# Merging logits and PV items of an attention stage by another weight

## The chip, the cores and the metric

The kernel runs on one core of a Trainium2 chip. The metric is the time of one execution in microseconds (us) on the device; of several executions the median counts. TensorE does the matmuls, VectorE, ScalarE and GpSimd the elementwise work, SyncE (SP) issues the DMAs.

## The reference: what is computed

One layer of a decoder on 2048 tokens of width 1024, with 16 learned meta tokens ahead of them. RMSNorm and one input projection feed three causal mixers: latent attention (MLA, 6 heads, keys of 64 + 32 rotary), differential attention (diff, 4 heads, two softmax maps of width 32 each per head, their weighted difference is applied to the values) and a sliding window of 128 (6 heads). Their outputs go through one output projection and the residual, then RMSNorm, a SwiGLU FFN of width 2816, the residual and a last RMSNorm:

```python
y = concat(mla(...), diff(...), swa(...))          # each (2048, heads * 64)
h = h + y @ w_out
h = h + (silu(n @ w_gate) * (n @ w_up)) @ w_down   # n = rms_norm(h)
out = rms_norm(h)[meta:]
```

For MLA and diff, a query row block of 128 attends to all key blocks up to its own, and to the meta tokens: softmax(q k + bias) v.

## The kernel before, in words

The program has four phases: phase_a projects, phase_b does MLA and diff attention, phase_o does the window attention and the output projection, phase_f the FFN. They overlap at their borders. Numbers are kept as pairs of a rounded part and its rest, so that two or three matmuls stand for one exact product.

**A unit of phase_b** is a pair of query row blocks (2g and 2g+1, g from 0 to 7) of one head. There are 48 MLA units; 32 diff units are spread over them, so that of three steps of the outer loop (`for j in range(48)`, end of phase_b) two carry a diff unit beside the MLA unit (a mixed unit below; unit 0 is the first step). Each unit gives two lists of work items, s1 (logits) and s2 (PV).

**Logits** (softmax_row). A row of 128 queries has its keys cut into pieces of 144 to 512 columns. For a piece, TensorE computes the logits into one of three PSUM buffers psS: three matmuls for MLA (lines 744 to 746), one for diff (line 802). VectorE then adds the bias, writes the piece into an SBUF tile p and keeps the running minimum mn (line 574), which frees psS. After a row's last piece ScalarE takes the exponentials of the whole row (line 579), and for diff GpSimd combines the two maps (lines 788 and 789). A diff unit has four such rows (two blocks, two maps), an MLA unit two. There are 12 p tiles.

**PV** (pv_pair). For two key blocks at a time TensorE transposes p into a PSUM buffer psTb (line 612, three buffers), ScalarE rounds it to pth (line 623) and VectorE forms the rest ptl (line 624); every third time ScalarE, then GpSimd do it (lines 619 to 621). Then TensorE multiplies both by the values into psO (line 642). A close folds and scales the sum (lines 649, 754, 755, 811 to 816) and stores y.

**Order.** PV of a unit is written into the program together with the logits of the next one. merge_to does it: each list's items have weights, and the list that is behind in its share of its own total gives the next item. With `merge(s1, prev)` the PV items of the unit before (prev) are so spread over the logits pieces. Of the PV items the weights are fixed (0.22 per transposed pair of blocks and the like). In a mixed unit, the rows of MLA and diff are first merged the same way, each row with the sum of its pieces' weights (rows_of, then merge_to).

The order written isn't yet the order that runs. The framework orders the instructions of each engine at build time along its own model of time (`TCKW = dict(schedule_with_timeline_sim=True)`, line 36): among those that the model holds ready, the one written first goes first.

Of the kernel before, what the change touches and what calls it, by code (L numbers as in the profile page):

```python
# [88 lines left out]
def key_chunks(m):  # L89

    out, c = [], 0
    for b in ([m] if m <= 8 else [-(-m // 2), m // 2]):
        w = b * P + (0 if c else META)
        n = -(-w // PW)
        pieces = []
        for j in range(n):
            k = (b // n + (1 if j >= n - b % n else 0)) * P + (0 if c else META)
            pieces.append((c, k))
            c += k
        out.append(pieces)  # L100
    return out
# [3 lines left out]
def trunk(ctx: ExitStack, tc: tile.TileContext, a, out):  # L105
# [408 lines left out]
    def phase_b(window):  # L514
        with ExitStack() as st:
# [28 lines left out]
            def softmax_row(items, i, mm_fn, cost, bias, fin):  # L544


                chunks = key_chunks(i + 1)
                last = chunks[-1][-1]
                st_ = {"n": 0, "p": []}

                def part(j, c0, w, e):
                    if e == 0:
                        st_["ps"] = psS.tile([P, PW], F32, name="psS")
                    ps = st_["ps"]
                    if w <= 512:
                        lo, hi = PW - 512, PW - 512 + w
                        mm_fn(ps[:, lo:hi], c0, w)
                    else:
                        w0 = w // 2 // 8 * 8
                        lo, hi = 512 - w0, 512 + w - w0  # L560
                        if e == 0:
                            return mm_fn(ps[:, lo:512], c0, w0)
                        mm_fn(ps[:, 512:hi], c0 + w0, w - w0)
                    n = st_["n"]
                    st_["n"] += 1
                    if n == 0:
                        st_["mn"] = sm.tile([P, 8], F32, name="mn")
                    mn = st_["mn"]
                    base = chunks[j][0][0]
                    if c0 == base:  # L570
                        st_["p"].append((base, chunks[j][-1][0] + chunks[j][-1][1] - base, pp.tile([P, CH], F32, name="p", bufs=NPB)))
                    p = st_["p"][j][2]
                    b = bias[:, 512 - w:512] if (c0, w) == last else zero.to_broadcast([P, w])
                    nc.vector.tensor_tensor_reduce(out=p[:, c0 - base:c0 - base + w], in0=ps[:, lo:hi], in1=b, scale=1.0,  # L574
                                                   scalar=mn[:, n - 1:n] if n else 3e38, op0=ALU.add, op1=ALU.min, accum_out=mn[:, n:n + 1])
                    if (c0, w) == last:
                        rsum = sm.tile([P, 2], F32, name="rsum")
                        for k, (_, m, x) in enumerate(st_["p"]):
                            nc.scalar.activation(out=x[:, 0:m], in_=x[:, 0:m], func=AF.Exp, bias=mn[:, n:n + 1], scale=-1.0, accum_out=rsum[:, k:k + 1])  # L579
                        if len(chunks) > 1:  # L580
                            nc.gpsimd.tensor_tensor(out=rsum[:, 0:1], in0=rsum[:, 0:1], in1=rsum[:, 1:2], op=ALU.add)
                        fin(st_["p"], rsum[:, 0:1])

                for j, pieces in enumerate(chunks):
                    for c0, w in pieces:
                        c = max(w, 256) * cost / 2400.0
                        if w > 512:
                            items.append((c / 2, lambda j=j, c0=c0, w=w: part(j, c0, w, 0)))
                            items.append((c / 2, lambda j=j, c0=c0, w=w: part(j, c0, w, 1)))
                        else:  # L590
                            items.append((c, lambda j=j, c0=c0, w=w: part(j, c0, w, 0)))
                items.append((0.0, lambda: None))
# [139 lines left out]
            def mla_unit(h, g, q, hf, kt, vt):  # L732
                s1, s2 = [], []
                rows, sums = [], []

                def fin(p, s):
                    rows.append(p)
                    sums.append(s)

                for i in (2 * g, 2 * g + 1):  # L740
                    o = slice((i - 4 * hf) * P, (i - 4 * hf + 1) * P)

                    def qk(s, c0, w, o=o):
                        nc.tensor.matmul(out=s, lhsT=q[:, 0, o], rhs=kt[:, c0:c0 + w], start=True, stop=False)
                        nc.tensor.matmul(out=s, lhsT=q[:, 1, o], rhs=kt[:, c0:c0 + w], start=False, stop=False)
                        nc.tensor.matmul(out=s, lhsT=q[:, 2, o], rhs=kr[:, c0:c0 + w], start=False, stop=True)

                    softmax_row(s1, i, qk, 3, ncaus[:, 4], fin)

                def out_y(yp):  # L750
                    y = tp.tile([P, 2, 64], F32, name="y")
                    r = sm.tile([P, 2], F32, name="ri")
                    for j in range(2):
                        nc.vector.reciprocal(out=r[:, j:j + 1], in_=sums[j])
                    nc.vector.tensor_tensor(out=y, in0=yp.rearrange("p (j d) -> p j d", j=2), in1=r.unsqueeze(2).to_broadcast([P, 2, 64]), op=ALU.mult)
                    nc.sync.dma_start(out=y_v[:, 2 * g:2 * g + 2, h * 64:(h + 1) * 64], in_=y)

                pv_pair(s2, g, rows, vt, out_y)
                return s1, s2
# [14 lines left out]
            def diff_unit(h, g, q, hf, kt, vt):  # L774
# [23 lines left out]
                for i in (2 * g, 2 * g + 1):  # L798
                    o = slice((i - 4 * hf) * P, (i - 4 * hf + 1) * P)
                    for m in range(2):  # L800
                        def qk(s, c0, w, o=o, m=m):
                            nc.tensor.matmul(out=s, lhsT=q[:, m, o], rhs=kt[m][:, c0:c0 + w], start=True, stop=True)  # L802
                        softmax_row(s1, i, qk, 1, ncaus[:, h], fin)
# [712 lines left out]
```

## Time and profile before

| | |
|---|---|
| median of 3 runs | 2818.74 us (2812.42 to 2819.20) |
| profiled execution | 2810.05 us |
| its span, first to last instruction | 2808.3 us |
| mean granted TensorE clock | 0.988 |
| TensorE busy with matmuls / loading weights | 2724.7 / 2339.2 us |
| VectorE, ScalarE, GpSimd busy | 1794.5, 1450.3, 1309.9 us |
| phase_b, first logits to first logits of unit 47 | 483 to 1105 us |

Busy time is the union of an engine's instructions. PE is TensorE's matmuls, PEld its weight loads, which overlap matmuls; DVE is VectorE, ACT ScalarE, POOL GpSimd. An idle stretch is put down to the instruction that released it: "PEld psS L802 <- DVE mn L574" is the weight load of line 802 that waited for line 574 on VectorE. Idle time of an engine costs something only where nothing else sets the pace there.

### The profile page before, as it was taken

What the parts mean: (1) busy time and instruction counts of PE and PEld (TensorE: products, weight loads), DVE (VectorE), ACT (ScalarE), POOL (GpSimd) and SP (SyncE); (2) the same over time, 40 slices, a digit from 0 to 9 for tenths busy, and PEclk for the clock granted to TensorE, in tenths of its full rate; (3) what the DMA queues carried; (4) which work ended last, traced back from release to release, by engine and by line L of the source; (5) the groups of instructions that cost most, each with busy time, mean ns of one, the idle gap of its engine ahead of it and who ended that gap; (6) DMA issues with size and microseconds to landing.
All of it is one profiled execution on the core that took longest, in us unless ns stands there. A gap on an engine that the chain in (4) does not pass through costs nothing.

```text
span 2808.3 us, 44596 instructions
## 1 busy us (share of the span) xinstructions
PE 2724.7 (97%) x14755; PEld 2339.2 (83%) x14755; DVE 1794.5 (64%) x4092; ACT 1450.3 (52%) x3264; POOL 1309.9 (47%) x1585
## 2 busy tenths in 40 slices
PE   8999999899999999899998999999999999999999
PEld 6888888888989899788886888887888888788887
DVE  6343333798988989655548666668766666655564
ACT  6444444788888888645444333334333333333343
POOL 1212122688887978512215555455654553222231
PEclk9999999899999999899999999999999999999999
DMA  7565456946464542667658333235322324834554
GB/s 198 144 179 141 136 145 170 246 99 152 117 159 101 135 100 66 187 180 212 182 170 263 107 104 109 90 98 202 113 96 95 107 91 140 309 120 144 174 189 147
DMA packets 418504, 415.53 MB, mean 148 GB/s; under 512 B 56426, under 2 KB 309328, under 8 KB 416352
## 3 DMA queue, kind: packets, MB, share of 16 engines
q1 hardware_dynamic: 418272, 412.67, 49.9%
q8 instruction: 117, 1.92, 0.3%
q14 instruction: 115, 0.94, 0.1%
HBM read 278.72 MB, written 137.18 MB: 148 GB/s over the span
## 4 chain that ended last, share of the span: by engine, by line
PE 81%; DMA 6%; DVE 4%; issue 4%; POOL 2%; ACT 2%; SPq 1%; POOLq 0%; DVEq 0%; ACTq 0%
PE ps L1225 10%; PE ps L1224 10%; PE ps L1223 10%; PE psO L642 5%; PE psA L123 4%; PE psTb L612 4%; PE psA L125 4%; PE psA L124 4%; PE ps L125 4%; PE ps L123 4%; PE ps L124 4%; PE psAo L123 2%; PE psAo L125 2%; PE psAo L124 2%; PE psS L802 2%
## 5 line engine op out<-in xcount | busy, mean ns | idle before, releaser
L1224 PE MATMUL ps<-x,wgh 128*128 128x512 f32 x1232 | 485.8, 395 | 4.8 <-DVE x L1193 4.8
L1223 PE MATMUL ps<-x,wgh 128*128 128x512 f32 x1232 | 483.6, 393 | 3.9 <-ACT x L1192 3.6
L1225 PE MATMUL ps<-x,wgl 128*128 128x512 f32 x1232 | 485.0, 394 | 2.2 <-DVE wgl L1215 2.2
L1155 POOL TENSOR_TENSOR wsum<-r 128x512 f32<-128x512 f32 x220 | 317.7, 1448 | 334.7 <-DVE wgl L1215 331.6
L579 ACT ACTIVATE p<-p,mn 128x656 f32<-128x656 f32 (+8 forms) x336 | 305.3, 914 | 34.9 <-DVE mn L574 30.3
L1214 ACT CAST wgh<-wsum 128x512 fp32r<-128x512 f32 x220 | 136.3, 620 | 311.0 <-PE ps L1224 199.3
L1224 PEld LDWEIGHTS ps<-x,wgh 128*128 128x128 f32 x1232 | 232.1, 188 | 61.7 <-DVE x L1193 8.8
L1223 PEld LDWEIGHTS ps<-x,wgh 128*128 128x128 f32 x1232 | 232.4, 189 | 57.9 <-ACT x L1192 4.4
L1225 PEld LDWEIGHTS ps<-x,wgl 128*128 128x128 f32 x1232 | 232.3, 189 | 53.8 <-DVE wgl L1215 2.6
L123 PE MATMUL ps<-bh,wgh 128*128 128x512 f32 x616 | 241.1, 394 | 2.6 <-ACT wgh L1360 2.6
L124 PE MATMUL ps<-bl,wgh 128*128 128x512 f32 x616 | 242.7, 394 | 0.0
L125 PE MATMUL ps<-bh,wgl 128*128 128x512 f32 x616 | 239.1, 395 | 0.0
L1215 DVE TENSOR_TENSOR wgl<-wsum,wgh 128x512 fp32r<-128x512 f32 x220 | 191.7, 872 | 58.8 <-ACT wgh L1214 57.5
L612 PE MATMUL psTb<-ident,p 128*128 128x128 f32 x1440 | 216.7, 276 | 3.5 <-DVE ptl L624 1.4
L123 PE MATMUL psA<-wi,xh 128*128 128x512 f32 (+2 forms) x528 | 203.4, 385 | 5.5 <-ACT wi L238 4.7
L1360 ACT CAST wgh<-wgl 128x512 fp32r<-128x512 f32 x154 | 95.0, 620 | 216.6 <-DMA wgl<-fd 180.9
L1361 DVE TENSOR_TENSOR wgl<-wgl,wgh 128x512 fp32r<-128x512 f32 x154 | 117.9, 773 | 132.6 <-ACT wgh L1360 127.9
L124 PE MATMUL psA<-wi,xh 128*128 128x512 f32 (+2 forms) x528 | 199.7, 378 | 0.4 <-DVE wi L239 0.3
L125 PE MATMUL psA<-wi,xl 128*128 128x512 f32 (+2 forms) x528 | 198.3, 376 | 0.0
L642 PE MATMUL psO<-pth,vt 128*128 128x256 f32 x720 | 193.4, 289 | 2.2 <-DMA vt<-vd 1.9
L642 PE MATMUL psO<-ptl,vt 128*128 128x256 f32 x720 | 194.1, 298 | 0.8 <-DVE ptl L624 0.2
L1155 POOL TENSOR_TENSOR hs<-c 128x512 f32<-128x512 f32 x108 | 154.9, 1441 | 61.5 <-DVE c L1314 51.9
(255 smaller groups left out, 6826.5 us busy)
## 6 DMA issues: line engine op xcount, KB each, us to landing
wgl<-fd SPq DMA_DIRECT2D x154, 256.0 KB, 3.4
fd<-hs SPq DMA_DIRECT2D x110, 256.0 KB, 2.8
qm<-qd SPq DMA_DIRECT2D x92, 256.0 KB, 5.0
r<-in_w_gate_dram SPq DMA_DIRECT2D x88, 256.0 KB, 4.1
r<-in_w_up_dram SPq DMA_DIRECT2D x88, 256.0 KB, 3.8
ws<-in_w_down_dram SPq DMA_DIRECT2D x77, 256.0 KB, 3.3
qd<-so SPq DMA_DIRECT2D x80, 192.0 KB, 2.0
qf<-qd SPq DMA_DIRECT2D x60, 256.0 KB, 5.6
```

Source lines behind the costliest of these rows:

```text
L123: nc.tensor.matmul(out=ps, lhsT=xh, rhs=wh, start=start, stop=False)
L124: nc.tensor.matmul(out=ps, lhsT=xh, rhs=wl, start=False, stop=False)
L125: nc.tensor.matmul(out=ps, lhsT=xl, rhs=wh, start=False, stop=stop)
L579: nc.scalar.activation(out=x[:, 0:m], in_=x[:, 0:m], func=AF.Exp, bias=mn[:, n:n + 1], scale=-1.0, accum_out=rsum[:, k:k + 1])
L612: nc.tensor.transpose(pt[:, j * 256 + q * P:j * 256 + (q + 1) * P], cols(rows[q], c), ident)
L642: nc.tensor.matmul(out=ot[:, 0:256], lhsT=v[:, vb], rhs=x, start=(st_["n"] == 1), stop=(st_["n"] == 2 * total))
L1155: eng.tensor_tensor(out=out, in0=x, in1=y, op=ALU.add if sign > 0 else ALU.subtract)
L1214: nc.scalar.copy(out=h, in_=src)
L1215: nc.vector.tensor_tensor(out=l, in0=src, in1=f32(h), op=ALU.subtract)
L1223: nc.tensor.matmul(out=ps, lhsT=h[:, k], rhs=o[:, 0, k], start=k == 0, stop=False)
L1224: nc.tensor.matmul(out=ps, lhsT=h[:, k], rhs=o[:, 1, k], start=False, stop=False)
L1225: nc.tensor.matmul(out=ps, lhsT=l[:, k], rhs=o[:, 0, k], start=False, stop=k == 3)
```

## The change

The weight of a piece of logits is no longer its time on TensorE (columns times matmuls, at 2400 per us, with at least 256 columns), but an amount 0.3 + w / 960 less that time (at 2300 per us), and at least 0.15. `cost` is 3 for MLA and 1 for diff. Nothing else changes.

```diff
@@ softmax_row
                 for j, pieces in enumerate(chunks):
                     for c0, w in pieces:
-                        c = max(w, 256) * cost / 2400.0
+
+                        c = max(0.3 + w / 960.0 - max(w, 256) * cost / 2300.0, 0.15)
                         if w > 512:
                             items.append((c / 2, lambda j=j, c0=c0, w=w: part(j, c0, w, 0)))
                             items.append((c / 2, lambda j=j, c0=c0, w=w: part(j, c0, w, 1)))
```

## Rows read from the trace of the kernel before

**Rows 1.** The page, part 1: busy time, share and instructions of each engine.
```profile
PE 2724.7 (97%) x14755; PEld 2339.2 (83%) x14755; DVE 1794.5 (64%) x4092; ACT 1450.3 (52%) x3264; POOL 1309.9 (47%) x1585
```

**Rows 2.** Busy times, 540 to 1105 us: columns as the header row says.
```profile
core 0: us, PE busy (x) PEld busy (x) DVE busy (x) ACT busy (x) POOL busy (x), PEclk, DMA share, GB/s
540.00:1105.00 565.00, 552.82 (x4029) 512.99 (x4028) 499.68 (x1774) 475.10 (x1146) 470.81 (x646) 1.00 0.50 123
```

**Rows 3.** Waits, 540 to 1105 us: waited for, us in total, times, longest.
```profile
DVE p L574 <- PE psS L746: 13.2, 27, 1.7
PEld psS L802 <- DVE mn L574: 11.8, 36, 0.8
PEld psS L744 <- DVE mn L574: 9.0, 24, 0.7
...
DVE p L574 <- PE psS L802: 7.4, 20, 0.9
...
DVE p L574 <- PE psTb L612: 6.0, 10, 1.4
```

**Rows 4.** Timeline of TensorE in unit 23: start, length, instruction, count.
```profile
782.86 0.34 PE L744 MATMUL psS<-kt,qm 128*128 128x384 f32 x1
783.03 0.34 PE L745 MATMUL psS<-kt,qm 128*128 128x384 f32 x1
783.21 0.34 PE L746 MATMUL psS<-kr,qm 128*128 128x384 f32 x1
783.39 0.28 PE L642 MATMUL psO<-zt,vt 128*128 128x256 f32 x1
783.50 1.04 PE L612 MATMUL psTb<-ident,p 128*128 128x128 f32 x8
784.29 0.42 PE L744 MATMUL psS<-kt,qm 128*128 128x384 f32 x1
```

**Rows 5.** Timeline of VectorE in unit 23.
```profile
790.38 0.62 DVE L574 CUSTOM_DVE_ANT_0 p<-psS,zero,mn 128x384 f32<-128x384 f32 x1
790.92 0.08 DVE L574 DVE_READ_ACCUMULATOR2_ANT mn<- 128x1 f32 x1
790.92 0.44 DVE L574 CUSTOM_DVE_ANT_0 p<-psS,zero 128x272 f32<-128x272 f32 x1
791.28 0.08 DVE L574 DVE_READ_ACCUMULATOR2_ANT mn<- 128x1 f32 x1
791.28 0.69 DVE L624 TENSOR_TENSOR ptl<-psTb,pth 128x512 fp32r<-128x512 f32 x1
```

**Rows 6.** Timeline of weight loads and matmuls at line 802, unit 23; idle before in brackets.
```profile
790.29 0.19 PEld L802 LDWEIGHTS psS<-kt,qf 128*128 128x128 f32 x1 [0.53 <-DVE mn L574]
791.06 0.19 PEld L802 LDWEIGHTS psS<-kt,qf 128*128 128x128 f32 x1 [0.58 <-DVE mn L574]
...
805.72 1.00 PE L802 MATMUL psS<-kt,qf 128*128 128x384 f32 x2 [0.48 <-DVE mn L574]
```

**Rows 7.** Timeline of TensorE in unit 24 and the start of unit 25.
```profile
809.60 0.31 PE L744 MATMUL psS<-kt,qm 128*128 128x144 f32 x1
...
809.98 0.61 PE L612 MATMUL psTb<-ident,p 128*128 128x128 f32 x4
810.35 0.36 PE L642 MATMUL psO<-ptl,vt 128*128 128x256 f32 x1
...
811.74 0.40 PE L642 MATMUL psO<-zt,vt 128*128 128x256 f32 x2
811.98 0.29 PE L744 MATMUL psS<-kt,qm 128*128 128x272 f32 x1
...
812.36 0.29 PE L744 MATMUL psS<-kt,qm 128*128 128x272 f32 x1
```

**Rows 8.** Waits of line 802 in units 11 (617:642), 23 (780:809), 35 (942:969).
```profile
PEld psS L802 <- DVE mn L574: 1.3, 5, 0.4
...
PEld psS L802 <- DVE mn L574: 2.8, 6, 0.7
...
PEld psS L802 <- DVE mn L574: 1.7, 3, 0.8
```

**Rows 9.** The grouped lines, whole span: busy us, mean ns, idle before.
```profile
L802 PE MATMUL psS<-kt,qf 128*128 128x384 f32 (+5 forms) x376 | 131.7, 387 | 4.6 <-DVE mn L574 3.6
...
L744 PE MATMUL psS<-kt,qm 128*128 128x384 f32 (+5 forms) x282 | 108.0, 383 | 11.5 <-DVE mn L574 4.3 <-issue 3.2 <-ACT qr L494 2.0
```

## The prediction

> **What bounds the kernel now.** I read the page's busy shares first [rows 1]: over the whole span TensorE is busy 97%, and nothing else comes near it. The change touches one stage, the attention of phase_b, so next I read the busy times of the stretch from 540 to 1105 us [rows 2]. It runs from within unit 5 to the end of unit 46 (the 48 units count from 0): before it the first keys still arrive, after it phase_o joins in. Here four engines are close together: of 565 us TensorE is busy 552.82, VectorE 499.68, ScalarE 475.10, GpSimd 470.81, at a granted clock of 1.00 (the 2.4 GHz level). DMA has half its share free. So this stage has no single bound; what it loses is lost where one engine waits for another.
>
> How much is that? Matmuls overlap, so their busy time hides short waits; the weight loads are busy 512.99 us, and 52 us lie between them. The rows of waits name two that go both ways [rows 3]. The weight load of a diff piece (line 802) waits 11.8 us in 36 places, that of an MLA piece (line 744) 9.0 us in 24, until VectorE has taken an earlier piece out of its psS buffer. And VectorE waits 13.2 and 7.4 us for the matmuls that fill one. That is the imbalance that the new weights aim at, and 20.8 us is about all that better merging can win on TensorE's side.
>
> Here the Trainium skill has a rule that would set another bound. Perfetto Trace Analysis, Identifying the Most-Contended Engine, says that matmul busy time is a poor measure of headroom and that the busy share of weight loads is to be used. By matmul busy time at most 12 us of this stretch could be won, by weight loads 52. The trace sides with the rule: at 790.29 and 791.06 the loads stand still for 0.53 and 0.58 us [rows 6].
>
> **The change part by part.**
>
> (1) *Weights.* No instruction is added or removed: 282 MLA pieces and 376 diff pieces stay [rows 9], with the same shapes and waits. What moves is the place of PV items (transposes, PV matmuls, closes) among them. For a piece of 384 columns the weight goes, for MLA, from 384 x 3 / 2400 = 0.48 to 0.3 + 0.4 - 0.501 = 0.199, and for diff from 0.16 to 0.3 + 0.4 - 0.167 = 0.533. PV is spread in proportion. I worked both merges through, item by item, with the old and the new weights: in the 32 units with a diff head (mixed units), 958 of 1656 transposes and PV matmuls are written behind an MLA piece and 698 behind a diff piece before; afterwards 302 and 1354.
>
> Is the new split the better one? An MLA piece of 384 occupies TensorE from 782.86 to 783.39, 0.53 us [rows 4]. VectorE starts such pieces 0.54 us apart when nothing holds it up (790.38 to 790.92 [rows 5]). So an MLA piece is even, while a diff piece takes a third of that on TensorE, 0.18 us, and leaves 0.36 us. PV of two key blocks takes four transposes at 0.10 (eight from 783.50 to 784.29 [rows 4]) and four matmuls at 0.12 (two from 811.74 to 811.98 [rows 7]), 0.9 us of TensorE, against 0.69 on VectorE [rows 5] in two of three cases (third: GpSimd). So the arithmetic of the new weights fits the trace.
>
> (2) *Does the written place decide?* This is the step on which the forecast turns. The queues are ordered at build time (line 36) among what the framework's model holds ready, the earliest written first. Unit 24 shows what this does: its two MLA pieces are of 144 and 272 columns, and nine transpose groups with their matmuls, some 7 us, are written between them; the trace has four transposes and 13 matmuls, then the 272, and at 812.36 already the next unit's first piece [rows 7]. Counted over phase_b from the order in the trace against the merge: the logits pieces run in the order written, all 658; a transpose runs 7.9 pieces later than written on average, a PV matmul 11.9. The new weights move a transpose by 0.6 pieces on average, at most 5. Of the 1454 transposes and 1532 PV matmuls that the 48 units' merges place, only 29 and 4 come to stand on the other side of the piece beside which they run. All others were written ahead of it already, weren't ready, and still are written ahead of it.
>
> So what the move wins directly: 33 instructions of about 0.11 us can fill a wait each, 3.6 us. Each could as well leave a wait where it stood before: 3.6 us lost is the bound on the other side. The far bound of a gain is all 20.8 us [rows 3], if the new ranks shift the queues of all engines. The few that change sides go mostly from MLA pieces to diff pieces, where TensorE waits, so I take the gain of 3.6.
>
> (3) *Order of rows.* Rows of MLA and diff are merged by the sums of these weights too. In 21 of the 32 mixed units the order stays (MLA, two diff, MLA, two diff). In nine (units 4, 11, 13, 20, 23, 35, 37, 44, 47) the third diff row now stands ahead of the second MLA row; in two (8, 32) it is the other way round. The nine shift 2+4+1+4+4+4+1+4+4 = 28 diff pieces from the second run of diff pieces to the first. Where no PV is ready, each of them costs TensorE 0.36 us, 10 us in all; where PV covers the first run and is used up in the second, the same 10 us are won. Units 11, 23 and 35 wait 1.3, 2.8 and 1.7 us at line 802 today, and unit 47 repeats the 2.8 of unit 23 [rows 8]; in unit 23 waits stand in the first run (790.29, 791.06) and in the second too (805.72) [rows 6]. I see no reason for either sign and take 0, keeping plus and minus 10 for the range.
>
> (4) *Loads and stores.* y is stored behind a close, on SP, in the same order; closes move by half a piece, under half a microsecond, and nobody waits for y before phase_o. Keys and queries are issued between units, which stay as they are. Their cover is the unit before; if it went, the price would be seen as waits of line 744 or 802 for a DMA, which the rows of waits don't have. PV that is written later holds its p tile longer; VectorE waits for transposes to free one for 6.0 us today [rows 3]. At half a piece more I take 0; the upper end is these 6.0 once more.
>
> **Sum.** -3.6 + 0 + 0: the profiled execution of 2810.05 us would become 2806.4. The median of the runs shown is 8.7 us above that execution, so I forecast 2815.1, 0.13% below 2818.74. A measurement of this kernel tells about 0.3% (8.5 us) from no change, so the forecast is "within 0.3%".
>
> **The rivals.**
>
> *Faster: the balance arrives.* If ranks shift on VectorE and ScalarE as well, diff pieces get PV between them, and the waits at 802 (11.8) vanish with half of those at 744 (4.5): 16 us, 2802. For it: both engines wait for each other in the same stretch. The Trainium skill speaks for it as well (Perfetto Trace Analysis, Optimization Strategy): where the most-contended engine changes between regimes, interleaving them may help. Against it: the 33 of 2986. Chance 0.33.
>
> *Slower: three diff rows in a run.* Place: the nine units, between the first and the second MLA row. Price: 28 pieces at 0.36, 10 us; with some of the 6.0 for p tiles, 2829 to 2831. It decides if PV isn't ready in the first run, because the p of the unit before is still with ScalarE's exponentials or GpSimd's combining. For it: unit 23's waits of 0.53 and 0.58 us stand in its first run [rows 6]. Against: the second run gets shorter by as much. Chance 0.21.
>
> *It doesn't do what it says:* the queues come out nearly as they are, because readiness orders them. That is the core of my forecast (0.46), and then the time is within 8.5 us of 2818.7. A rule of the Trainium skill points there as well: a repeating gap on the engine that should be saturated can mean too few buffers (Perfetto Trace Analysis, Optimization Strategy). Three psS buffers are what the waits at 744 and 802 are for, and by that rule the gaps stay whatever the weights; no run here shows another number of buffers.
>
> **How the numbers follow.** Forecast 0.46, faster 0.33, slower 0.21; these are the chances of the three classes. The low end is all 20.8 us won, 2798, and a microsecond for the scatter of the runs: 2797. The high end is 2831, the slower rival with p tiles. Because no case reaches beyond these unless new waits appear, I leave about 2 in 10 outside.
>
> **What would show it.** Right: pieces from 540 to 1105 take the same stretch within 6 us; VectorE's, ScalarE's and GpSimd's busy times there are unchanged; the waits at 744 and 802 sum to 15 to 22 us. The balance rival: the wait at 802 falls below 5 us and VectorE's idle time of 65 us shrinks with it. The slower rival: the wait at 802 rises in the nine units (first in units 23 and 47, above 4 us). I am wrong in step 2 if the PV transposes stand elsewhere among the pieces by several places on average, and wrong in step 4 if phases behind phase_b change their length by more than 3 us.

## The result and the profile after

The changed kernel takes 2829.28 us (median of 6 runs, 2825.33 to 2832.63), the kernel before on the same chip 2816.47 (6 runs): a ratio of 1.0056, 95% interval 1.0045 to 1.0068. It is slower by 0.56%, 12.8 us. The time lies in the predicted range, but the forecast itself, 0.13% faster and "within 0.3%" (chance 0.46), missed; "slower" had 0.21. The profiled execution of after took 2828.42 us, with a span of 2826.6, and lies near its median.

The page's busy times answer to [rows 1]:

```profile
PE 2729.7 (97%) x14755; PEld 2345.7 (83%) x14755; DVE 1794.2 (63%) x4092; ACT 1454.7 (51%) x3264; POOL 1312.9 (46%) x1585
```

Every count is the same. TensorE's busy time rose by 5.0 us for the same instructions, the span by 18.3. The same piece of phase_b, from within unit 5 to the end of unit 46, answers to [rows 2]. Columns: stretch, length, busy time and count of each engine, granted clock, DMA share, GB/s.

```profile
core 0: us, PE busy (x) PEld busy (x) DVE busy (x) ACT busy (x) POOL busy (x), PEclk, DMA share, GB/s
542.00:1117.00 575.00, 556.04 (x4036) 516.06 (x4035) 500.30 (x1780) 477.89 (x1149) 473.34 (x647) 1.00 0.49 120
```

It is 10 us longer for nearly the same work (seven more matmuls fall into it). From the first logits of unit 6 to those of unit 47 the delay grows by 8.3 us, in a second profile by 9.1. TensorE's busy time rose by 3.2 us, VectorE's by 0.6, ScalarE's by 2.8, GpSimd's by 2.5: the rest is idle time of all four. Its waits answer to [rows 3] (in after, lines behind 586 have numbers one higher: line 744 is now L745, 802 is L803, 612 is L613):

```profile
DVE p L574 <- PE psS L747: 16.3, 29, 1.7
PEld psS L803 <- DVE mn L574: 14.2, 35, 0.7
DVE p L574 <- PE psS L803: 9.1, 21, 1.4
PEld psS L745 <- DVE mn L574: 7.2, 24, 0.6
DVE p L574 <- PE psTb L613: 6.3, 7, 2.8
PEld psO L643 <- POOL pth L621: 2.8, 2, 2.6
PE psS L745 <- DMA qm<-qd: 1.4, 1, 1.4
```

The waits that the change aims at are the same sum as before: 14.2 + 7.2 = 21.4 us against 11.8 + 9.0 = 20.8. What is new is at the bottom, and small in number: a wait of 1.4 us for a DMA (before has one of 0.4 us in this stretch, at line 746, which [rows 3] leave out), one long wait for GpSimd's pth, and a longest wait of VectorE for a p tile of 2.8 us (1.4 before).

**Where the time went.** The first logits of each unit can be found in TensorE's timeline, and so the delay against the first profile of before. One profile can mislead, so before and after were each profiled twice:

| delay in us at | unit 0 | 24 | 25 | 27 | 34 | 35 | 47 | first output projection | end |
|---|---|---|---|---|---|---|---|---|---|
| after, first | 1.9 | 2.7 | 3.3 | 7.7 | 7.3 | 11.4 | 11.8 | 15.8 | 18.3 |
| after, second | 0.5 | -0.1 | 0.1 | 4.6 | 4.2 | 9.4 | 9.7 | 14.3 | 13.6 |
| before, second | -0.3 | 1.1 | 1.1 | 1.1 | 1.1 | 1.1 | 1.0 | 2.2 | 0.7 |

So it isn't a slow drain over 48 units. There are two steps, of 4.4 to 4.5 us between units 25 and 27 and of 4.1 to 5.2 between units 34 and 35, and a third part of 4 to 6.5 us behind unit 47. The second profile repeats both steps within 1.1 us.

### The profile page after: what moved, and what is told of

It is laid out like the page before. It is cut to its first block, busy times and chain, and to the rows that moved or that the text cites. A ratio compares the mean times of both kernels' runs of the same rounds, so it can differ in the third digit from the quotient of the medians.

```text
span 2826.6 us, 44602 instructions
## 1 busy us (share of the span) xinstructions
PE 2729.7 (97%) x14755; PEld 2345.7 (83%) x14755; DVE 1794.2 (63%) x4092; ACT 1454.7 (51%) x3264; POOL 1312.9 (46%) x1585
## 4 chain that ended last, share of the span: by engine, by line
PE 82%; DMA 5%; DVE 5%; issue 3%; POOL 2%; ACT 2%; SPq 1%; POOLq 0%; DVEq 0%; ACTq 0%
PE ps L1226 10%; PE ps L1225 10%; PE ps L1224 10%; PE psO L643 5%; PE ps L123 4%; PE ps L124 4%; PE ps L125 4%; PE psTb L613 4%; PE psA L123 4%; PE psA L125 4%; PE psA L124 4%; DVE p L574 2%; PE psAo L123 2%; PE psAo L125 2%; PE psAo L124 2%
## 5 line engine op out<-in xcount | busy, mean ns | idle before, releaser
L1226 PEld LDWEIGHTS ps<-x,wgl 128*128 128x128 f32 x1232 | 232.1, 188 | 53.7 <-DVE wgl L1216 2.6
L613 PE MATMUL psTb<-ident,p 128*128 128x128 f32 x1440 | 219.1, 277 | 4.0 <-POOL p L790 1.7
```

What stands on the lines that cost most here:

```text
L613: nc.tensor.transpose(pt[:, j * 256 + q * P:j * 256 + (q + 1) * P], cols(rows[q], c), ident)
L1226: nc.tensor.matmul(out=ps, lhsT=l[:, k], rhs=o[:, 0, k], start=False, stop=k == 3)
```

## Experiments

All ran on one core, beside the kernel before on the same chip; the ratio is to that kernel's runs, with its 95% interval. A delay is told as in the table above.

### Which of the two merges does it

The weights enter two merges: that of PV items with pieces, and that of the rows of MLA and diff. A number that carries a second value splits them (`new` and `old` stand for the two lines of the diff above). e1_pv uses the new weights for PV and the old sums for the rows; e2_rows the other way round.

```diff
+class W(float): pass
-                out.append((sum(c for c, _ in cur), cur))
+                out.append((sum(getattr(c, 'row', c) for c, _ in cur), cur))
-                        c = max(w, 256) * cost / 2400.0
+                        c = W(new); c.row = old      # e1_pv;   e2_rows: c = W(old); c.row = new
```

> The pieces of logits carry the new weights where PV is merged among them; the rows of MLA and diff are merged by the old sums, so the order of rows is that of before. Theory A (the order of rows costs the time): within 4 us of before, and TensorE's waits in units 6 to 46 as before, since TensorE's queue comes out the same up to the last unit. Theory B (PV beside diff pieces instead of MLA pieces costs the time): 10 to 14 us slower than before. Theory C (any change of the written order shuffles the queues and costs or gains by chance): anything from -10 to +14 us.

> The other half: PV is merged by the old weights, the rows of MLA and diff by the new sums, so that 11 units have the changed order of rows. Theory A: 10 to 14 us slower than before, like the changed kernel. Theory B: within 4 us of before. Theory C: anything from -10 to +14 us, not tied to the changed kernel's time.

Measured: e1_pv 1.0019 [1.0009, 1.0030], e2_rows 1.0037 [1.0023, 1.0050]. Together 0.56%, the whole change. e1_pv's 0.19% is 5 us, a little more than theory A allowed; e2_rows' 0.37% is 10 us, at the lower edge of its range.

The queues that come out of the build tell more than the times. In e1_pv 480 of 922 PV items are written elsewhere, and TensorE's queue is that of before, instruction by instruction, until unit 47. Unit 47 starts 0.1 us late; the loss is behind it, where its PV meets phase_o: the two queues first differ at 1139.8 us. So up to there the written place of a PV item decides nothing, since the framework orders the queues itself. The order of the rows does: it fixes the order of the logits, and all that follows is arranged around it. In e2_rows both steps of after are there: unit 27 is late by 3.7 us, unit 34 by 5.3, unit 35 by 9.4, unit 47 by 11.4. Its profiled execution, the fastest of its runs (2815.82 us against a median of 2820.27), ends only 5.7 us late: behind unit 47 one execution says little.

### Unit 23 alone, and a third buffer for the queries

e8_row23 merges the rows by the new sums in unit 23 only (its third diff row comes ahead of the second MLA row); all else is as before, with the number of two values of e2_rows, of which rows_of takes the second where its new argument is true. e13_row23_q3 is that with a third buffer for MLA's query tile qm.

```diff
-                    merge_to(t1, rows_of(s1), rows_of(e1))
+                    merge_to(t1, rows_of(s1, j in (23,)), rows_of(e1, j in (23,)))
# e13_row23_q3 also:
-                    q = qp.tile([P, 3, SEQ // 4], F32R, name="qm")
+                    q = qp.tile([P, 3, SEQ // 4], F32R, name="qm", bufs=3)
```

> Old weights, and the changed order of rows in unit 23 alone (third diff row ahead of the second MLA row). TensorE's queue differs from before only from within unit 23 to unit 24. Theory A1 (unit 23's order delays the p tiles and query loads of units 24 to 26): units 23 to 26 take 4 to 6 us more in the profile, and the run is 3 to 6 us slower. Theory A2 (the order costs only where several changed units follow each other): units 23 to 26 within 1.5 us, the run within 3 us.

> Unit 23's changed row order (the kernel of the run e8) with a third buffer for MLA's queries (tile qm); the queues of the four compute engines come out the same as in that run, but for 12 rows of TensorE's, and only SP's differs. Theory Q (the second MLA row, now behind a third diff row, frees its query buffer later, so the queries of unit 25 land when TensorE already waits for them, and the clock falls after that wait): the wait of line 744 for the DMA at the start of unit 25 (2.8 us) is gone, the granted clock stays at 1.00 through units 24 and 25, and units 23 to 26 take at most 1.5 us more than before: the run is within 2 us of before. If the order itself costs: 4 to 6 us more, as in e8.

Measured: e8_row23 1.0015 [1.0006, 1.0023], with a step of its own: unit 24 is 0.9 us early, unit 25 0.7 late, unit 26 4.5, unit 27 6.2, and 6.4 still at unit 47. Here is how it comes about. First before: the last matmul of unit 23's second MLA row on TensorE, and the load that it lets go, on SP's queue.

```profile
800.35 0.40 PE L746 MATMUL psS<-kr,qm 128*128 128x512 f32 x1
...
800.97 0.58 SPq L708 DMA_DIRECT2D qm<-qd  x1
```

The same two in e8_row23, and the first logits of unit 25, which read that load:

```profile
805.23 0.39 PE L746 MATMUL psS<-kr,qm 128*128 128x512 f32 x1
...
805.84 0.58 SPq L708 DMA_DIRECT2D qm<-qd  x1
...
813.10 0.57 PE L744 MATMUL psS<-kt,qm 128*128 128x272 f32 x1 [2.77 <-DMA qm<-qd]
```

MLA's queries sit in two tiles. The load for unit 25 may overwrite unit 23's, so SP waits for the last matmul of unit 23 that reads it: 0.22 us pass from that matmul's end to the issue in both kernels (800.75 to 800.97, 805.62 to 805.84). The third diff row in front of the second MLA row moves that end back by 4.9 us. The Trainium skill (DMA: Bandwidth & Descriptors, Anatomy of one DMA — SWDGE (gpsimd) path) says that a DMA engine waits on no semaphore and that the wait is held by the issuing sequencer; for these loads, which SP issues, the two rows agree. Unit 24 is short [rows 7], and TensorE arrives at unit 25 2.77 us too early.

From unit 23's first logits to unit 27's it is 63.6 us before and 69.5 in e8_row23, so 5.9 us are lost, and this wait is about half of them. Most of the rest is the clock. The same stretch by busy time, before and then e8_row23:

```profile
core 0: us, PE busy (x) PEld busy (x) DVE busy (x) ACT busy (x) POOL busy (x), PEclk, DMA share, GB/s
810.90:817.70 6.80, 6.80 (x56) 6.64 (x55) 5.39 (x19) 6.76 (x19) 5.44 (x7) 1.00 1.07 273
```

```profile
810.90:817.70 6.80, 4.60 (x20) 4.54 (x21) 1.76 (x9) 3.23 (x9) 5.71 (x6) 0.50 1.01 222
```

From 810.9, within the wait, the granted clock is 0.50 for 6.8 us (the 1.2 GHz level), and then 1.00 again. Before, it is 1.00 throughout. Of the 6.8 us 2.2 still belong to the wait; in the other 4.60 TensorE is busy, and at half the clock half of that, 2.3 us, is lost. 2.77 + 2.3 = 5.1. The Trainium skill (TensorE: Matmul & The Clock Gate, Part 1) says that the throttled state is the default and that the engine's activity releases it; a fall to 0.50 within the wait and a return to 1.00 behind 4.60 us of work agree.

With the third buffer e13_row23_q3 measures 0.9990 [0.9981, 0.9999]. No wait for qm is left, and from before the place of the fall to behind it the clock is full:

```profile
806.00:824.00 18.00, 16.37 (x117) 14.70 (x117) 12.53 (x47) 14.00 (x38) 16.70 (x21) 1.00 0.95 240
```

Unit 27 is 0.4 us early instead of 6.2 late. From unit 23's first logits to unit 27's it takes 64.4 us: 5.1 less than e8_row23, which is the wait and the clock's part, and 0.8 more than before. The compute engines run nearly the queues of e8_row23 (five of TensorE's matmuls stand elsewhere, at the wait itself), so it was the load. This settles the first step for unit 23 alone.

The third buffer by itself and under the changed kernel:

```diff
# e15_before_q3: before;   e14_after_q3: after
-                    q = qp.tile([P, 3, SEQ // 4], F32R, name="qm")
+                    q = qp.tile([P, 3, SEQ // 4], F32R, name="qm", bufs=3)
```

> The changed kernel with the third query buffer; compute queues the same as the changed kernel's. Theory Q: its wait for queries at unit 25 (1.4 us) goes, but the step at units 34 and 35 and that of the last unit stay, as they don't wait for queries: 3 to 5 us faster than the changed kernel, so 0.35 to 0.45% above before. If queries are all of it: within 3 us of before.

> The kernel before with the third query buffer; compute queues the same as before's. Theory Q: within 3 us of before (0 to 3 us faster), as its queries land in time but for the 0.4 us at line 746. If the buffer helps by itself: 3 us or more faster.

Measured: e15_before_q3 0.9990 [0.9981, 0.9998], e14_after_q3 1.0033 [1.0022, 1.0045]. In after the buffer takes back 0.23 of 0.56%, but not the whole first step: units 25 to 27 still lose 4.2 us, by a second wait. (From unit 23 to 27 it is 3.8 us, against 5.7 and 5.3 in the two profiles of after.) In after itself both stand in TensorE's timeline, and the clock behind them in the windows:

```profile
815.68 0.36 PE L745 MATMUL psS<-kt,qm 128*128 128x272 f32 x1 [1.44 <-DMA qm<-qd]
...
823.63 0.39 PE L643 MATMUL psO<-pth,vt 128*128 128x256 f32 x1 [2.32 <-POOL pth L621]
```

```profile
824.90:828.30 3.40, 3.40 (x15) 3.40 (x15) 1.95 (x11) 0.98 (x5) 3.40 (x3) 0.50 0.84 296
```

What holds up that pth is to be read one engine at a time, VectorE first and then GpSimd:

```profile
818.15 0.44 DVE L574 CUSTOM_DVE_ANT_0 p<-psS,zero 128x272 f32<-128x272 f32 x1 [2.75 <-PE psTb L613]
...
820.09 0.27 DVE L787 TENSOR_SCALAR cf<-rsum,rd,nlam 128x1 f32<-128x1 f32 x1
```

```profile
820.46 2.24 POOL L789 TENSOR_SCALAR p<-p,cf 128x1040 f32<-128x1040 f32 x2 [2.60 <-DVE ri L755]
...
822.96 0.62 POOL L621 TENSOR_SCALAR pth<-ptx 128x512 fp32r<-128x512 f32 x1
```

VectorE stands 2.75 us, at its end for a p tile; up to 816.68 it had no logits either, as the queries came late. Behind the pieces in its queue is the small cf of the diff rows, GpSimd stands 2.60 us until cf is there (the row names ri, VectorE's next instruction at that moment; cf is what it reads), and the pth that TensorE wants is queued behind GpSimd's 2.24 us of combining. This looks like one stall that is handed on from engine to engine. It isn't. With a third query buffer TensorE's wait for pth is all that is left of its two, it is as long as in after, and the clock falls all the same:

```profile
819.36 0.58 PE L642 MATMUL psO<-pth,vt 128*128 128x256 f32 x1 [2.32 <-POOL pth L620]
```

```profile
818.90:825.70 6.80, 6.34 (x26) 6.17 (x27) 4.50 (x19) 1.49 (x7) 6.80 (x6) 0.50 0.90 242
```

But VectorE's stall at the same piece is 0.71 us now (0.68 in before), and GpSimd stands 0.55 us in front of its combining:

```profile
813.88 0.44 DVE L574 CUSTOM_DVE_ANT_0 p<-psS,zero 128x272 f32<-128x272 f32 x1 [0.71 <-PE psTb L612]
...
816.19 2.24 POOL L788 TENSOR_SCALAR p<-p,cf 128x1040 f32<-128x1040 f32 x2 [0.55 <-DVE ri L754]
...
818.69 0.62 POOL L620 TENSOR_SCALAR pth<-ptx 128x512 fp32r<-128x512 f32 x1
```

What stays is the order in GpSimd's queue, the pth behind the combining. In before the same two instructions stand the other way round, and TensorE doesn't wait:

```profile
812.14 0.64 POOL L620 TENSOR_SCALAR pth<-ptx 128x512 fp32r<-128x512 f32 x1
...
815.55 2.24 POOL L788 TENSOR_SCALAR p<-p,cf 128x1040 f32<-128x1040 f32 x2
```

So the second wait was built into GpSimd's queue when the order of the rows changed. This is read from the three profiles; the two instructions were not exchanged by themselves.

### One more p tile

Step 4 of the prediction had a term of up to 6.0 us for p tiles. e11_after_13p gives after 13 of them, e12_before_13p before.

```diff
-CH, NPB, PW, NPS, NPT, NPO = 1040, 12, 512, 3, 3, 2
+CH, NPB, PW, NPS, NPT, NPO = 1040, 13, 512, 3, 3, 2
```

> The changed kernel with 13 p tiles in place of 12. Theory P (the new order holds p tiles longer, VectorE waits for one, and the cost is that wait): VectorE's waits for transposes at line 574 fall by more than half in units 23 to 26, and the run is 4 us or more faster than the changed kernel (2829 us, 0.56% above before). If p tiles are not the cause: within 3 us of the changed kernel, beside what a 13th tile gives the kernel before.

> The kernel before with 13 p tiles: what the tile gives by itself. Theory P: 0 to 3 us faster, as VectorE waits only 6.0 us for p tiles there. Theory C: a shuffle, -5 to +10 us.

Measured: 1.0049 [1.0035, 1.0063] and 1.0004 [0.9994, 1.0014]. In the profile of e11_after_13p the wait for pth at unit 25 is gone, and the one for the queries is longer:

```profile
816.19 0.36 PE L744 MATMUL psS<-kt,qm 128*128 128x272 f32 x1 [3.47 <-DMA qm<-qd]
```

The step at units 34 to 35 is gone as well (5.3 us late, then 4.8), and unit 47 is late by 4.5 us instead of 9.7 to 11.8. Yet the ratio is only 0.07% better than after's, within the intervals and less than the 4 us of theory P, and the profiled execution ends 14.2 us late: what phase_b gets back is lost again behind unit 47. Nor does the tile as such show as the cause. With 13 tiles the queues come out of the build otherwise (at 2991 of TensorE's 14755 places another matmul stands than in after), and GpSimd's pth is ahead of the combining again (816.14 and 820.99 us). Before loses 7.7 us behind unit 47 with 13 tiles too, in its one profile, which was the slowest of its runs (2820.41 us).

### Units 32 and 35

e9_rows32_35 takes the new order of rows in these two units alone. As it had the step at units 34 to 35, e16_row32 and e17_row35 then took them apart. In unit 32 the new order is the opposite kind: an MLA row moves ahead of diff rows.

```diff
-                    merge_to(t1, rows_of(s1), rows_of(e1))
+                    merge_to(t1, rows_of(s1, j in (32, 35)), rows_of(e1, j in (32, 35)))   # e9; e16: (32,); e17: (35,)
```

> Old weights, and the changed order of rows in units 32 and 35 alone. Theory A1 (each changed unit costs by itself): units 32 to 37 take 4 to 6 us more. Theory A2: within 1.5 us. In either case the last unit is left as before; Theory C (the end of the stage, where unit 47 meets the windows of phase_o, shuffles with any change ahead of it) has phase_o longer or shorter by 3 to 9 us, though nothing in it was changed.

> Old weights; the rows are merged by the new sums in unit 32 alone, where the order goes the other way (the second MLA row ahead of a diff row, instead of behind it). Theory (the step of 4 to 5 us at the change from unit 34 to 35 comes from unit 32, whose PV shift runs on through the units behind it): the first logits of unit 35 come 4 to 6 us later against before, those of unit 34 within 1 us, and the run takes 4 to 8 us longer, ratio 1.0015 to 1.003. Rival (unit 35's own order makes it): unit 35 starts within 1 us of before and the ratio is 0.999 to 1.001.

> Old weights; the rows are merged by the new sums in unit 35 alone (its third diff row ahead of the second MLA row). Theory (unit 32 makes the step): units 32 to 36 start within 1 us of before, ratio 0.999 to 1.001. Rival (unit 35's own order makes it, by what its pieces wait for): unit 36 starts 3 to 6 us later than before, ratio 1.001 to 1.003. If neither this one nor unit 32 alone shows the step, it takes both.

Measured: e9_rows32_35 1.0033 [1.0020, 1.0046], e16_row32 1.0059 [1.0046, 1.0073], e17_row35 1.0016 [1.0007, 1.0026]. As to the step, the theory holds: in e16_row32 unit 34 starts 1.4 us early and unit 35 2.7 late, a step of 4.1; in e17_row35 units 34 and 35 keep the same -0.7. (Its 0.16% lies in the rival's range, but unit 36 comes only 1.1 us later, at 0.4, and not 3 to 6.) As to the run it misses: unit 32 alone costs as much as the whole change, more than the 1.003 expected, and with unit 35 beside it less. The parts don't add.

The step itself has no long wait. TensorE's timeline of e16_row32 shows the end of a PV chain with no logits written between:

```profile
935.76 0.38 PE L642 MATMUL psO<-ptl,vt 128*128 128x256 f32 x1 [0.69 <-POOL ptl L621]
937.56 0.66 PE L649 MATMUL psO<-fold,os 128*128 128x64 f32 x4 [0.94 <-ACT os L647]
```

After has the same two at 944.44 and 946.26 (0.67 and 0.97 us). From unit 32's first logits to unit 47's TensorE is busy 191.23 of 199.5 us in e16_row32, 192.81 of 196.6 before: 8.3 us idle against 3.8, in many short pieces. Which of these the new order causes directly was not taken further.

Most of what unit 32 costs lies behind unit 47, so before, after and e16_row32 were profiled again, unchanged.

> The kernel before once more, for a second profile. Question for the three: which part of a difference seen behind unit 47 belongs to the order of the instructions and comes again, and which is the scatter of one execution. Theory (the queues set the waits up to unit 47, and behind it loads of rows from DRAM come in by chance of the moment): all units start within 1 us of the first profile; from window row 0 on the second profile may differ from the first by up to 7 us. Rival (every profile of one kernel is alike to the end): the ends differ by under 2 us.

> The kernel after once more. Theory: its steps at units 24 to 27 (4 to 5 us) and 34 to 35 (4 us), and the 11 to 12 us at unit 47, come again within 1.5 us, and with them the wait of 1.4 us for the queries and of 2.3 us for pth; the part behind unit 47 (6.5 us in the first profile) may be anything from 0 to 12. Rival: the steps in phase_b are scatter too and one of them is missing.

> The row order of unit 32 alone once more. Its median is 17 us above before, its first profile 10 us (3 at unit 47, counted from the same start). Theory: the step at units 34 to 35 (4 us) comes again, and most of the rest lies behind unit 47: end 12 to 20 us above before. Rival: the rest lies before unit 47, which then starts 8 us or more late.

The second profile of before ends 0.7 us from its first and lies within 2.5 of it at every place looked at. That of after is the second row of the table above; it has the wait for the queries (1.0 us) and for pth (2.33) again. r3_row32 starts unit 47 late by 2.0 us (1.6 in e16_row32) and ends late by 17.0 (10.0). So much of the cost lies behind unit 47 both times, and the same two waits are there; their sizes stray from one execution to the next. In e16_row32, ScalarE and then TensorE:

```profile
1176.92 0.62 ACT L1010 CAST woh<-r 128x512 fp32r<-128x512 f32 x1 [3.21 <-DMA r<-in_w_out_dram]
```

```profile
1181.10 0.69 PE L939 MATMUL psOo<-pth,vw 128*128 128x384 f32 x1 [4.39 <-ACT pth L932]
...
1214.43 0.63 PE L1037 MATMUL psX<-ident,yt 128*128 128x128 f32 x4 [4.09 <-DMA yt<-yd]
```

and in r3_row32 again:

```profile
1182.20 0.69 PE L939 MATMUL psOo<-pth,vw 128*128 128x384 f32 x1 [5.03 <-ACT pth L932]
...
1216.59 1.09 PE L1037 MATMUL psX<-ident,yt 128*128 128x128 f32 x4 [4.61 <-DMA yt<-yd]
```

ScalarE stands 3.21 us before a cast of output weights that haven't come yet; the window's pth, for which TensorE waits 4.39, comes behind it. In both profiles of before the first of these two matmuls doesn't wait, and the second waits 0.54 and 0.59 us. Later in SP's queue the store of y that the next load of yt stands behind is issued 5.7 us later than before. SP in before, then in e16_row32:

```profile
1200.50 0.32 SPq L954 DMA_DIRECT2D yd<-yw  x1
1202.22 0.32 SPq L1021 DMA_DIRECT2D yt<-yd  x1
```

```profile
1206.20 0.32 SPq L954 DMA_DIRECT2D yd<-yw  x1
...
1207.93 0.53 SPq L1021 DMA_DIRECT2D yt<-yd  x1
```

From 1170 to 1230 TensorE is busy 54.8 and 53.7 us of 60 in the two profiles of before, 48.0 and 45.8 in those of unit 32 alone. That one wait follows from the other was read from the rows, not tried by itself.

### The other eight units

e10_others takes the new order in units 4, 8, 11, 13, 20, 37, 44 and 47.

```diff
-                    merge_to(t1, rows_of(s1), rows_of(e1))
+                    merge_to(t1, rows_of(s1, j in S), rows_of(e1, j in S))   # S = (4, 8, 11, 13, 20, 37, 44, 47)
```

> Old weights; the changed row order in units 4, 8, 11, 13, 20, 37, 44 and 47, so all of the eleven but 23, 32 and 35. If the cost of the row order sits in units 23 and 32 to 35 alone (they gave +4.3 and +7.2 us): within 3 us of before. If each of the longer runs of diff rows costs (the slower rival of the prediction, 0.36 us a piece, 20 of its 28 pieces are here): 5 to 8 us slower.

Measured: 1.0013 [1.0004, 1.0022], 3.7 us, between the two expectations. Eight units, seven of them with the same kind of move as unit 23, cost no more together than unit 23 alone. So the move has no fixed price; what counts is what is due when it is made.

### Other weights

e3_floor drops the 256 columns' floor (9 other units change their rows); e5_vec weighs a piece by VectorE's time in full (7 units do); e18_vec_q3 is e5_vec with the third query buffer.

```diff
-                        c = max(w, 256) * cost / 2400.0
+                        c = w * cost / 2400.0          # e3_floor
+                        c = 0.3 + w / 960.0            # e5_vec, e18_vec_q3 (with bufs=3 for qm)
```

> The old weight without its floor of 256 columns (w * cost / 2400): a change that means nothing for the balance of the engines, but moves a row in 9 units (1, 2, 8, 13, 16, 25, 32, 37, 40), mostly to MLA, diff, diff, MLA, diff, diff or one place off it. Theory A in its strong form (a third diff row ahead of the second MLA row costs): only units 13 and 37 or none have it, so within 5 us of before. Theory B: PV stays beside MLA pieces, so within 4 us of before. Theory C: off by 5 us or more in either direction.

> Weight of a piece is VectorE's time alone (0.3 + w / 960), the same for MLA and diff: a third of PV is written behind MLA pieces (586 of 1656), and rows change in 7 units (2, 4, 8, 13, 25, 32, 37), not in the units with g of 5 to 7 (11, 20, 23, 35, 44, 47). Theory A: 4 to 9 us slower if units 13, 25 and 37 carry the cost, about 0 if the long rows of units 11, 20, 23, 35, 44 and 47 do. Theory B: 5 to 10 us slower, in proportion to the PV moved. Theory C: anything.

> All weights 0.3 + w / 960 (VectorE's time in full, nothing taken off for TensorE), and a third buffer for MLA's queries. If the two effects add (the weight alone gave 0.9995, the third buffer alone 0.9990): ratio 0.998 to 0.999, 3 to 5 us faster than before. Rival (the two act on the same few waits, or neither does more than the scatter of the runs): 0.999 to 1.000, no gain that can be told.

Measured: e3_floor 1.0046 [1.0031, 1.0061], e5_vec 0.9995 [0.9986, 1.0003], e18_vec_q3 0.9983 [0.9975, 0.9992] (2806.83 us against 2811.87). Dropping the floor costs almost as much as the change. It shifts rows in nine units, and four of them (2, 13, 25 and 37), not two, get a third diff row ahead of the second MLA row; which shift costs wasn't taken apart. e5_vec shifts rows too, unit 32 in the same way as e16_row32, and the run costs nothing. From unit 32's first logits to unit 47's it takes 2.6 us more than before, e3_floor 2.7, e16_row32 3.0. So about 3 us come with this order of unit 32 in three builds; the rest of e16_row32's 0.59% lies behind unit 47 and doesn't come with the order as such. e18_vec_q3 is faster than both kernels, though by less than the 0.3% that was set as the bound; that its two parts add is likely by the intervals, not shown (0.05 + 0.10 against 0.17%). Its profiled execution, 2811.02 us, was the longest of its runs and doesn't show where the gain is.

## Why the prediction was wrong

**What bounds the kernel** held. No engine's work grew by more than a few us, and the loss is idle time of engines that wait for each other, and matmuls at half the clock behind it.

**(1) Weights** held as arithmetic, and was beside the point: the waits that the weights were to even out are 21.4 us now, in the band of 15 to 22 given for "right", although the pieces take 8 to 10 us more where at most 6 was given. That band alone would have passed a kernel that is slower.

**(2) Does the written place decide?** "No" was right, and stronger than argued: e1_pv's queue is that of before up to unit 47. But the count of 33 instructions failed as a measure of what moves. It compared the written places with the old trace, with everything else held still. In the trace of after 870 of 1520 transposes and 940 of 1600 PV matmuls run beside another piece than before, up and down alike (by 1.1 and 1.3 pieces; on average 0.1 and 0.4 earlier). These moves follow from the order of rows (in e2_rows 824 and 919 move, in e1_pv none), which step 2 did not ask about. The gain of 3.6 us isn't to be seen.

**(3) Order of rows** is the step that failed first. "I see no reason for either sign and take 0", with 0.36 us for each piece that loses or finds its PV. The size of the range (10 us) was near, but not by that price: the waits of line 802 rose by 2.4 us in all. What the move costs depends on what is due then. In unit 23 the row's end lets a query load go: 5.1 of 5.9 us are that wait and the clock behind it. Unit 32, which the step named and did not price, costs as much by itself as the whole change, mostly behind unit 47 and by waits whose origin is open. The step also misread its own rows. Of the 21 mixed units that keep their order, ten already have three diff rows ahead of the second MLA row, as have units 8 and 32 before the change: the price of such a run stood in the trace of before, where these twelve units wait 4.3 us at line 802 and the other twenty 10.4. And the nine third rows have 33 pieces, not 28 (five in each of units 11, 23, 35 and 47, three in unit 4), 11.9 us by the step's own price.

**(4) Loads and stores** is where the mechanism was missed. "Keys and queries are issued between units, which stay as they are. Their cover is the unit before", it says. It names the sign to look for, a wait of line 744 for a DMA, and that is what came: 2.77 us in e8_row23, 1.0 to 1.4 in after. The instruction that issues the load stays where it is, but it waits for a buffer, and its last reader moved by 4.9 us. The cover is counted from there. That could be read before: with two qm tiles and one in use by unit 24, a load for unit 25 cannot start before unit 23's last MLA row ends, and [rows 7] show that unit 24 is the short one. For p tiles the term of 0 held: VectorE's wait for them hardly rose (6.3 us against 6.0; 4.6 in e14_after_q3, where the queries come in time). What the step had no term for is the place of a pth in GpSimd's queue, 2.32 us of TensorE's time. "Nobody waits for y before phase_o" said nothing of phase_o itself: the phases behind unit 47 now lose 4 to 6.5 us in the two profiles, more than the 3 that the prediction set as the sign of an error here.

**A term that the sum didn't have** is the clock. The stretch was read at a granted clock of 1.00, so every wait was priced at its length. At a wait of 2.3 to 2.8 us the clock fell to 0.50 for 3.4 or 6.8 us, which in e8_row23 added 2.3 us to the 2.77 of the wait.

**The rivals.** The slower one had the sign and the time (2829 to 2831), but that is luck, for its cause isn't there: three diff rows in a run starve nobody at line 802. In units 23 and 47, where it asked for waits above 4 us, they fell from 2.8 us each to 1.6 and 1.2, and in all nine units from 7.9 to 6.8. The faster one fails: the waits at 802 rose. "It doesn't do what it says" holds for PV items and fails for rows.

## What to carry to other kernels

Where a scheduler orders the queues at build time, ask of a weight which orders it fixes for good (here that of the rows) and which it only suggests (the PV items): compare the built queues with one of the two undone. Price a moved block by what its last instruction lets go, a buffer whose next load or store waits in another engine's queue, and count the cover from that release, not from the place of the load. Compare the queues of the other engines too: an item that TensorE waits for can have come to stand behind a longer one. Reorderings of this stage cost from nothing (e5_vec) to 0.59% (e16_row32), so try such an edit in halves, and look for one or two steps rather than for a loss spread over all units.

## What the runs showed that was not expected

- A wait of 2.77 us within dense work went with 6.8 us at a granted clock of 0.50, one of 2.32 us with 6.8 (e14_after_q3) and 3.4 (after). The two waits of 0.69 and 0.94 us in e16_row32 had none behind them, but in e9_rows32_35 the same two did, in this window:

```profile
939.20:942.60 3.40, 3.20 (x15) 3.20 (x16) 2.36 (x8) 1.45 (x4) 3.02 (x5) 0.50 0.09 19
```

  The second profile of after has such a fall at the same place (from 943.9 us, 3.4 us long). With it the step at units 34 to 35 is 5.1 (e9_rows32_35) and 5.2 us, without it 4.1 (e16_row32, first profile of after).

- The moves of single units don't add: unit 32 alone 0.59%, units 32 and 35 together 0.33%.
- Two profiles of one kernel repeat its steps in phase_b within about 1 us, but can differ by 7 us at the end (10.0 and 17.0 for unit 32 alone). Behind unit 47 single profiles served to find waits; the costs were taken from the medians. What of after's own 4 to 6.5 us there comes from which wait stays open.
